# Low pieces of 23 operand blocks made beside attention and kept in DRAM, and the last product of attention's first pair in a bank of its own

## The chip, the cores and the metric

The kernel runs on one core of a Trainium2 chip. The metric is the device time of one execution in microseconds. The kernel before took 1278.0 us, the median of three runs (1276.09 to 1281.77).

## The reference

One decoder layer on a sequence of 1024 tokens with 1024 channels, all in float32. A single projection feeds two branches, the recurrence (Mamba-2) and forgetting attention; each branch goes through a 1024x1024 weight, the two are merged by gates, and the merged result goes through an output weight.

```python
h = _rmsnorm(x, pre_g)
proj = jnp.einsum('bld,de->ble', h, w_in)
z_ssm, xbc, dt_raw, q, k, v, f_raw, z_att, g_ssm, g_att = jnp.split(proj, _offsets(IN_SPLITS), axis=-1)
...
y_ssm = (yg.reshape(bsz, seqlen, SSM_D_INNER) * ssm_norm_g.astype(f32)).astype(x.dtype)
...
o = _forgetting_attention(heads(q), heads(k), heads(v), log_f)
o = o.transpose(0, 2, 1, 3).reshape(bsz, seqlen, ATT_D)
y_att = (o.astype(f32) * jax.nn.silu(z_att.astype(f32))).astype(x.dtype)
p_ssm = jnp.einsum('ble,ed->bld', y_ssm, w_branch_ssm)
p_att = jnp.einsum('ble,ed->bld', y_att, w_branch_att)
merged = jax.nn.sigmoid(g_ssm) * p_ssm + jax.nn.sigmoid(g_att) * p_att
out = jnp.einsum('bld,de->ble', merged, w_out)
return x + _rmsnorm(out, post_g)
```

## The kernel before

Every large matrix product is done by a seven-product scheme (Strassen and Winograd's). The activations, 1024 channels by 1024 tokens, are cut into four blocks of 512x512, b11, b12, b21 and b22, and from these come t1 = b12 - b11, t2 = b22 - t1, t3 = t2 - b11 and t4 = t2 - b21. Seven operands meet the weights: b11, b21, -b22, t1, -t2, t3, t4, held in SBUF as tiles x0 to x6 in this order. Each operand has four tiles of 128x512 (j = 0 to 3). TensorE multiplies in float32r, so each operand tile is split in two: a high piece (x3h, a rounded copy made by ScalarE) and a low piece (x3l, what the rounding lost, made by VectorE). One product is 4 x 3 = 12 matmuls of 128x512: high by high, high by low, low by high.

A `Pair` (L320) is two units of 128 output columns that share the seven products. Its steps have the numbers 1 to 7: step 1 uses b11 (x0), 2 b21 (x1), 6 -t2 (x4), 5 t1 (x3), 7 t3 (x5), 4 t4 (x6), 3 -b22 (x2). Steps 1, 6, 7 and 4 accumulate one after another into one PSUM bank, `self.b`; after 1, 6 and 7 ScalarE copies the bank to SBUF (`keep`, L399) before the next step may go on in it, because the sums in between are wanted too. `give` (L405) combines a bank with such a copy. `Stream` (L461) holds one list of steps for all 48 pairs: 36 of the input projection, then 4 of the recurrence's branch (weights `wbs`, operands `ops_s`), 4 of attention's branch (`wba`, `ops_a`) and 4 of the output weight (`ops_w`). A step is issued in two halves, and between halves the other work of the program is put: first the recurrence, then attention.

Attention (from L1322) runs 48 groups of 128-query blocks beside the stream: scores on TensorE (`s`), VectorE adds the forget gate and takes the row limit (`ex`, `nm`, L1505), ScalarE exponentiates (L1509), TensorE transposes (`pt`), ScalarE, for some tiles VectorE, copies that to SBUF (`p`, L1548 and L1546), TensorE multiplies by the values (`av`). Beside it, small steps called chores are taken from a line, one at each half.

`Operands.differences` (L197) is such a line of chores for `ops_s`: for each j it loads blocks of the recurrence's output, GpSimd subtracts (L211), and t1 to t4 are stored to DRAM on GpSimd's queue (L193). When a pair that uses other operands is next, `some` (L294) loads the new operands tile by tile (`fetch`, L257) into the low piece's place, and splits them (`split`, L265: ScalarE at L275 or L278, then VectorE at L276 or L279). For the output weight's operands t3, t4 and b22 the low pieces are already made early and kept in DRAM (`lows`): there `fetch` loads both pieces and `split` has only ScalarE's rounding in place (L269). Attention's own differences are made where its outputs appear (`outputs`, L1575). The last head pair's tiles are split straight from SBUF (`put`, L287).

`gp`, the pool of `small()` tiles (name `th`), has four buffers that go round among gates, loads and stores. The order on TensorE is that of the program; on the other engines a scheduler sets the order, except where `pin` keeps it.

## Time and profile before

| what | us |
|---|---|
| median of three runs | 1278.0 |
| the profiled execution | 1273.87 |
| its span | 1272.2 |
| TensorE busy | 1246.1 |
| VectorE busy | 1012.9 |
| ScalarE busy | 794.3 |
| GpSimd busy | 319.3 |

Attention lies between about 682 and 1122 us from the start of the span. The operands of the recurrence's branch are exchanged between about 918 and 977 us, those of attention's branch between about 1067 and 1130 us, those of the output weight between about 1170 and 1205 us. In a row of a view, `[0.69 <-ACT s L402]` means that the engine sat idle for 0.69 us before this instruction, until ScalarE's instruction at line 402 released it. PE is TensorE, PEld its weight loads, DVE VectorE, ACT ScalarE, POOL GpSimd, SP the engine that issues most loads. TensorE's matmuls overlap in the pipeline and their ends are modelled, so a product is best timed from start to start.

### The profile page before, as it was taken

How to read it: one execution, taken by the hardware profiler on the slowest of the kernel's cores; microseconds unless marked ns; L12 is line 12 of the kernel's file. 1: busy time of each engine (PE TensorE's matmuls, PEld its weight loads, DVE VectorE, ACT ScalarE, POOL GpSimd, SP SyncE). 2: the span in 40 equal slices, each digit the busy share in tenths (PEclk: the TensorE clock that was granted, in tenths of full speed). 3: DMA queues.
4: the chain of work that ended last, by engine and by line, in shares of the span. 5: the costliest groups of instructions: out<-in, count | busy, mean ns of one | idle time of the engine just before them, and what ended most of it. 6: DMA issues, size and time to landing. Idle time of an engine off the chain costs nothing.

```text
span 1272.2 us, 20822 instructions
## 1 busy us (share of the span) xinstructions
PE 1246.1 (98%) x6926; PEld 982.3 (77%) x6926; DVE 1012.9 (80%) x1994; ACT 794.3 (62%) x1737; POOL 319.3 (25%) x322
## 2 busy tenths in 40 slices
PE   5999999999999999999999999999999999999997
PEld 3678888888888888888887777777777777778886
DVE  7988886988888978997767676767789767886975
ACT  7745665556665765566555666666687666844753
POOL 4000440013400241115102124223112212356062
PEclk9999999999999999999999999999999999999999
DMA  8232452545436533744447576666687657766933
GB/s 300 69 120 76 146 162 88 191 152 182 138 101 215 175 127 117 219 146 140 142 149 252 162 228 212 217 214 218 232 286 263 224 184 249 249 221 199 364 110 105
DMA packets 152236, 233.56 MB, mean 184 GB/s; under 512 B 15201, under 2 KB 60737, under 8 KB 152129
## 3 DMA queue, kind: packets, MB, share of 16 engines
q1 hardware_dynamic: 136064, 196.08, 47.7%
q10 hardware_dynamic: 10560, 18.06, 3.8%
q0 software_dynamic: 5504, 18.09, 3.7%
q8 instruction: 54, 0.88, 0.3%
q14 instruction: 54, 0.43, 0.1%
HBM read 162.99 MB, written 72.34 MB: 185 GB/s over the span
## 4 chain that ended last, share of the span: by engine, by line
PE 86%; DMA 4%; DVE 4%; ACT 4%; issue 1%; SPq 0%; POOL 0%; DVEq 0%; ACTq 0%; POOLq 0%
PE pb L128 36%; PE pc L128 21%; PE pd L128 7%; PE av L128 5%; PE pt L131 5%; PE s L128 5%; PE yps L128 2%; PE st L128 1%; ACT ex L1509 1%; DMA xt<-in_x 1%; PE tr L131 1%; PE tr_v L131 1%; DMA v<-v_dram 1%; PE df L128 1%; DVE wop L350 1%
## 5 line engine op out<-in xcount | busy, mean ns | idle before, releaser
L350 DVE TENSOR_TENSOR wop<-sum,wop 128x512 fp32r<-128x512 f32 x180 | 140.2, 780 | 53.6 <-ACT wop L349 52.6
L349 ACT ACTIVATE wop<-sum 128x512 fp32r<-128x512 f32 x180 | 112.5, 626 | 109.0 <-DVE sum L355 52.4
L1509 ACT ACTIVATE ex<-ex,nm 128x512 f32<-128x512 f32 (+1 forms) x192 | 116.2, 606 | 71.9 <-DVE nm L1505 71.6
L402 ACT ACTIVATE s<-pb 128x512 f32<-128x512 f32 x144 | 85.3, 593 | 98.2 <-PE pb L128 96.2
L128 PE MATMUL pb<-x0h,wop 128*128 128x512 f32 x384 | 131.5, 399 | 0.0
L128 PE MATMUL pb<-x6h,wop 128*128 128x512 f32 x384 | 129.5, 395 | 1.3 <-ACT s L402 1.3
L128 PE MATMUL pb<-x5h,wop 128*128 128x512 f32 x384 | 130.1, 396 | 0.7 <-ACT s L402 0.7
L350 DVE TENSOR_TENSOR wop<-raw,wop 128x512 fp32r<-128x512 f32 x144 | 105.4, 733 | 31.8 <-ACT wop L349 31.5
L128 PE MATMUL pc<-x3h,wop 128*128 128x512 f32 x384 | 129.8, 396 | 0.5 <-DVE ot L419 0.4
L128 PE MATMUL pc<-x2h,wop 128*128 128x512 f32 x384 | 130.2, 397 | 0.0
L128 PE MATMUL pb<-x4h,wop 128*128 128x512 f32 x384 | 129.1, 395 | 0.0
L1505 DVE CUSTOM_DVE_ANT_0 ex<-s,fb 128x512 f32<-128x512 f32 (+1 forms) x192 | 96.8, 552 | 20.0 <-PE s L128 14.8
L349 ACT ACTIVATE wop<-raw 128x512 fp32r<-128x512 f32 x144 | 89.7, 623 | 14.7 <-PE pd L128 6.1
L128 PE MATMUL pd<-x1h,wop 128*128 128x512 f32 x288 | 96.3, 394 | 0.0
L128 PEld LDWEIGHTS pb<-x6h,wop 128*128 128x128 f32 x384 | 72.1, 188 | 18.6 <-issue 2.0
L128 PEld LDWEIGHTS pb<-x5h,wop 128*128 128x128 f32 x384 | 72.1, 188 | 18.4 <-issue 2.0
L128 PEld LDWEIGHTS pb<-x0h,wop 128*128 128x128 f32 x384 | 72.6, 189 | 17.6 <-issue 2.9
L128 PEld LDWEIGHTS pc<-x3h,wop 128*128 128x128 f32 x384 | 72.1, 188 | 17.7 <-issue 1.5
L128 PEld LDWEIGHTS pc<-x2h,wop 128*128 128x128 f32 x384 | 72.1, 188 | 17.4 <-issue 2.4
L128 PEld LDWEIGHTS pb<-x4h,wop 128*128 128x128 f32 x384 | 72.1, 188 | 16.7 <-issue 1.9
L211 POOL TENSOR_TENSOR wd<-wd 128x256 f32<-128x256 f32 x32 | 32.4, 1011 | 205.0 <-DMA wd<-in_wo 135.0
L131 PE MATMUL pt<-ident,ex 128*128 128x128 f32 x576 | 75.1, 273 | 2.0 <-ACT ex L1509 1.4
(318 smaller groups left out, 2993.6 us busy)
## 6 DMA issues: line engine op xcount, KB each, us to landing
raw<-in_wu SPq DMA_DIRECT2D x128, 256.0 KB
csb<-cs_dram SPq DMA_DIRECT2D x32, 256.0 KB
q<-q_dram SPq DMA_DIRECT2D x32, 256.0 KB
k<-k_dram SPq DMA_DIRECT2D x16, 512.0 KB
fb<-f_dram SPq DMA_DIRECT2D x16, 512.0 KB
rb<-st_dram SPq DMA_DIRECT2D x48, 128.0 KB
wd<-in_wo SPq DMA_DIRECT2D x40, 128.0 KB
xt<-in_x SPq DMA_DIRECT2D x8, 512.0 KB
```

Source lines behind the costliest of these rows:

```text
L128: return tc.keep_in_program_order(nc.tensor.matmul(*args, **kw))
L131: return tc.keep_in_program_order(nc.tensor.transpose(out_, in_, idn))
L211: pin(nc.gpsimd.tensor_tensor(t[out_], t[a_], t[b_], ALU.subtract))
L349: nc.scalar.activation(op[:, 0], src, AF.Copy)
L350: nc.vector.tensor_tensor(op[:, 1], src, op[:, 0], ALU.subtract)
L402: nc.scalar.activation(s, ps, AF.Copy)
L1505: nc.vector.tensor_tensor_reduce(o, s[e][:, 0:w], fb[hp, h][:, e, 0:w], 1.0, 3.0e38, ALU.add, ALU.min, nm)
L1509: pin(nc.scalar.activation(o, o, AF.Exp, scale=-1.0, bias=nm, accum_out=hd.at(hd.sm, i, h, e)))
```

## The change

Three edits. First, `ops_s` keeps low pieces of t1, t3, t4 and b22 (16 tiles), and `ops_a` those of t1 and t4 (seven tiles; the eighth, of the last head pair, is still split from SBUF). A new function `lower` makes them where the difference is at hand: ScalarE rounds into a `small()` tile, VectorE subtracts in place, GpSimd's queue stores it. A tile counts as ready once its low piece is stored. Second, `fetch` then loads two tiles for each of these, and `split` does ScalarE's rounding in place alone. Third, in attention's first pair step 7 gets a PSUM bank of its own: it doesn't wait for the copy of the sum of steps 1 and 6; VectorE adds that copy afterwards in `keep`, and step 4 goes on in the new bank and is combined in `give`.

The edit of `p.bank` for pairs behind that one has no effect: the banks of the last eight pairs are set anew behind attention, before these use them.

```diff
@@ class Operands
-            self.lows = {}
+            self.lows, self.late = {}, ()
         def ready(self, name, j):
-            if name in self.BLOCKS:
+            if name in self.BLOCKS and name not in self.late:
                 r, h = self.BLOCKS[name]
                 return self.there(KH * r + j, h)
             return (name, j) in self.made
         def store(self, name, j, t, cols=slice(0, HALF)):
             pin(self.queue.dma_start(self.dram[name][j][:, cols], t))
-            if cols.stop == HALF:
+            if cols.stop == HALF and name not in self.late:
                 self.made.add((name, j))
+        def lower(self, name, j, t):
+            s = small()
+            pin(nc.scalar.activation(s.bitcast(F32R), t, AF.Copy, scale=-1.0 if name == "b22" else 1.0))
+            if name == "b22":
+                pin(nc.vector.scalar_tensor_tensor(s.bitcast(F32R), t, -1.0, s, ALU.mult, ALU.subtract))
+            else:
+                pin(nc.vector.tensor_tensor(s.bitcast(F32R), t, s, ALU.subtract))
+            pin(self.queue.dma_start(self.lows[name][j], s))
+            self.made.add((name, j))
@@ differences
             wait = (None,) * room
+            if self.late:
+                part = lambda name, t: lambda: self.lower(name, j, state[t])
+                behind = lambda *fns: lambda: [fn() for fn in fns]
+                yield from (start, *wait, less("t1", "x", "x", "y"), keep("b22"), part("t1", "x"), None)
+                yield from (behind(part("b22", "y"), less("t2", "x", "y", "x")), keep("b11"), *wait)
+                yield from (less("t3", "y", "x", "y"), keep(), part("t3", "y"), lambda: fetch("b21"), *wait)
+                yield from (less("t4", "x", "x", "y"), keep(), part("t4", "x"))
+                return
@@ split
-            if name.strip("-") in self.lows:
+            if raw is None and name.strip("-") in self.lows:
@@ class Pair
+            self.apart = None
+        def another(self):
+            pool, tag = self.room
+            return pool.tile([P, HALF], F32, tag=tag, bufs=1, name="p" + tag)
-        def keep(self, ps):
+        def keep(self, ps, more=None):
             s = wp.tile([P, HALF], F32, tag="s", bufs=3, name="s")
             with tc.high_priority():
+                if more is not None:
+                    nc.vector.tensor_tensor(s, ps, more, ALU.add)
+                    return s
                 nc.scalar.activation(s, ps, AF.Copy)
@@ give
-                else:
+                elif how == "from":
                     nc.vector.tensor_tensor(d, s, ps, ALU.subtract)
+                else:
+                    nc.vector.scalar_tensor_tensor(d, ps, -1.0, s, ALU.mult, ALU.subtract)
@@ do
-                    yield from self.matmuls(self.b, 7, "t3", False)
-                    self.k7 = self.keep(self.b)
+                    if self.apart == 7:
+                        self.b = self.another()
+                    yield from self.matmuls(self.b, 7, "t3", self.apart == 7)
+                    self.k7 = self.keep(self.b, self.k2 if self.apart == 7 else None)
...
-                yield from self.matmuls(self.b, 4, "t4", False)
-                self.give(1, 0, self.b)
+                if self.apart == 4:
+                    self.b = self.another()
+                yield from self.matmuls(self.b, 4, "t4", self.apart == 4)
+                self.give(1, 0, self.b, {7: self.k2, 4: self.k7}.get(self.apart), "neither")
@@ class Stream
-                p.bank, p.other = (pj, "be"[n % 2]), (pjx, "d") if n < double else (pj, "c")
+                p.bank, p.other = (pj, "be"[(n + (n > last)) % 2]), (pjx, "d") if n < double else (pj, "c")
             a, b, c, d, e, f, g, h = pairs[last:]
+            a.apart, a.room = 7, (pj, "be"[(last + 1) % 2])
@@ the operands
+    ops_a.late = ("t1", "t4")
+    ops_a.lows = {n: tc.dram_tile([KH, P, HALF], F32, name=f"{n}_low_a") for n in ops_a.late}
+    ops_s.late = ("t1", "t3", "t4", "b22")
+    ops_s.lows = {n: tc.dram_tile([KH, P, HALF], F32, name=f"{n}_low_s") for n in ops_s.late}
@@ outputs
-                        stream.chores += [None, lambda: ops_a.store("t1", hp, y)]
+                        stream.chores += [None, lambda: ops_a.store("t1", hp, y), lambda: ops_a.lower("t1", hp, y)]
...
-                stream.chores += [None, lambda: ops_a.store("t4", j, x)]
+                stream.chores += [None, lambda: ops_a.store("t4", j, x), lambda: ops_a.lower("t4", j, x)]
```

The scheduled program changes from attention on; up to there every engine has the same instructions in the same order. Three places show how.

ScalarE, where the recurrence's operands are exchanged (x5 is t3 and x3 is t1 of `ops_s`; the line numbers of the changed kernel are higher). Before:

```order
L278 ACTIVATE x5h<-x5l 128x512 x2
L1509 ACTIVATE ex,sm<-ex,nm 128x512 x2
L1509 ACTIVATE ex,sm<-ex,nm 128x384
L413 ACTIVATE th<-pb 128x512
L349 ACTIVATE wop<-raw 128x512
L1509 ACTIVATE ex,sm<-ex,nm 128x384
L278 ACTIVATE x5h<-x5l 128x512 x2
L629 ACTIVATE th<-th 128x512
L278 ACTIVATE x3h<-x3l 128x512
L1431 ACTIVATE st<-pt 8x128
L1548 ACTIVATE p<-pt 128x2x128
L278 ACTIVATE x3h<-x3l 128x512
```

Now:

```order
L288 ACTIVATE x5h<-x5h 128x512 x2
L1547 ACTIVATE ex,sm<-ex,nm 128x512 x2
L1547 ACTIVATE ex,sm<-ex,nm 128x384 x2
L288 ACTIVATE x5h<-x5h 128x512 x2
L440 ACTIVATE th<-pb 128x512
L369 ACTIVATE wop<-raw 128x512
L1469 ACTIVATE st<-pt 8x128
L1586 ACTIVATE p<-pt 128x2x128
L1586 ACTIVATE p<-pt 128x512 x2
L663 ACTIVATE th<-th 128x512
L288 ACTIVATE x3h<-x3h 128x512 x2
```

The roundings are as many as before, but the second exponential of 384 columns no longer stands behind a gate's copy and a weight's rounding, and the copies `p` stand ahead of the roundings of x3.

ScalarE in attention's early part, where the first low piece is made (L200 is the rounding in `lower`). Before:

```order
L349 ACTIVATE wop<-sum 128x512
L1431 ACTIVATE st<-pt 8x128
L629 ACTIVATE th<-th 128x512
L1432 DMA st_dram<-st 8x128
L1548 ACTIVATE p<-pt 128x512
```

Now:

```order
L369 ACTIVATE wop<-sum 128x512
L663 ACTIVATE th<-th 128x512
L664 DMA gs_dram<-th 128x512
L200 ACTIVATE th<-x 128x512
L1469 ACTIVATE st<-pt 8x128
L1470 DMA st_dram<-st 8x128
L1586 ACTIVATE p<-pt 128x512
```

A rounding now stands ahead of a copy `p`. Of the 23 new roundings 12 stand ahead of a copy `p` with no exponential between.

TensorE at the end of attention, where step 6 (x4) of attention's first pair is followed by step 7 (x5). Before, the last row of step 6 and the first of step 7:

```order
L128 MATMUL pb<-x4h,wop 128x512
L128 MATMUL pb<-x5h,wop 128x512
L128 MATMUL pb<-x5l,wop 128x512
L128 MATMUL pb<-x5h,wop 128x512 x2
L128 MATMUL pb<-x5l,wop 128x512
```

Now:

```order
L128 MATMUL pb<-x4h,wop 128x512
L128 MATMUL pe<-x5h,wop 128x512
L128 MATMUL pe<-x5l,wop 128x512
L128 MATMUL pe<-x5h,wop 128x512 x2
L128 MATMUL pe<-x5l,wop 128x512
```

TensorE's order is the same; only the bank of steps 7 and 4 is another.

More of the change, by code (lines that the diff above doesn't have):

```diff
@@ L417, in give @@
                     nc.vector.tensor_tensor(d, ps, s, ALU.subtract)
+                elif how == "from":
+                    nc.vector.tensor_tensor(d, s, ps, ALU.subtract)
                 else:
-                    nc.vector.tensor_tensor(d, s, ps, ALU.subtract)
+                    nc.vector.scalar_tensor_tensor(d, ps, -1.0, s, ALU.mult, ALU.subtract)
             post(ch)
```

## The prediction

> **What bounds the kernel now.** I read the page first, busy time and the chain of work that ended last, then the busy time by stretch, then the waits of TensorE, and last the timeline where TensorE stood still.
>
> ```profile
> PE 1246.1 (98%) x6926; PEld 982.3 (77%) x6926; DVE 1012.9 (80%) x1994; ACT 794.3 (62%) x1737; POOL 319.3 (25%) x322
> PE 86%; DMA 4%; DVE 4%; ACT 4%; issue 1%; SPq 0%; POOL 0%; DVEq 0%; ACTq 0%; POOLq 0%
> 1142.50 8.16 PE pb L128 x36
> ```
>
> TensorE is busy for 98% of the span and holds 86% of the chain. The third row, from the chain in order of time, gives its pace: 36 matmuls in 8.16 us, 2.72 us a product. The change leaves the number and the order of matmuls alone, so it can win only where TensorE waits, and lose only by new waits of TensorE. The busy time by stretch shows where it waits (columns: PE, PEld, DVE, ACT, POOL busy, granted clock, DMA share, GB/s):
>
> ```profile
> 683.00:945.00 262.00, 261.24 (x1768) 198.39 (x1764) 188.22 (x505) 175.47 (x445) 68.55 (x86) 1.00 0.64 213
> 945.00:960.00 15.00, 13.73 (x85) 9.05 (x85) 14.73 (x34) 11.71 (x28) 2.15 (x4) 1.00 0.98 352
> 960.00:980.00 20.00, 19.62 (x128) 14.61 (x125) 18.25 (x46) 15.88 (x40) 4.68 (x6) 1.00 0.69 228
> 1105.00:1125.00 20.00, 18.72 (x103) 13.69 (x104) 18.66 (x38) 15.54 (x36) 6.98 (x6) 1.00 0.72 231
> 1125.00:1150.00 25.00, 25.00 (x112) 20.72 (x111) 20.25 (x23) 8.78 (x16) 18.28 (x13) 1.00 0.57 178
> ```
>
> In the 262 us of attention ahead of the exchange of operands TensorE stands for 0.76 us. It stands for 1.27 and 0.38 us at the exchange to the recurrence's branch, where VectorE is busy 98% and 91% of the time, and for 1.28 us at attention's end. Behind that it doesn't stand at all. The reader is to see that both places are where VectorE is full, and that the prize is small: 2.93 us of visible idle time.
>
> A busy TensorE can hide a little more. The timeline, with TensorE and its weight loads, shows it:
>
> ```profile
> 951.29 0.14 PEld L131 LDWEIGHTS pt<-ident,ex 128*128 128x128 f32 x1 [0.39 <-DVE nm L1505]
> 953.69 0.53 PEld L131 LDWEIGHTS pt<-ident,ex 128*128 128x128 f32 x5 [1.17 <-ACT ex L1509]
> 955.76 2.87 PE L128 MATMUL s<-k,q 64*128 64x512 f32 x12
> 977.26 0.30 PEld L128 LDWEIGHTS s<-k,q 64*128 64x128 f32 x4 [0.82 <-DVE p L1546]
> 1095.46 1.50 PE L128 MATMUL s<-k,q 64*128 64x512 f32 x12
> 1112.96 0.19 PEld L128 LDWEIGHTS pc<-x3l,wop 128*128 128x128 f32 x1 [0.66 <-DVE x3l L279]
> 1113.90 0.19 PEld L128 LDWEIGHTS pc<-x3l,wop 128*128 128x128 f32 x1 [0.41 <-DVE x3l L279]
> 1120.45 0.19 PEld L128 LDWEIGHTS pb<-x5h,wop 128*128 128x128 f32 x1 [1.11 <-ACT s L402]
> ```
>
> The twelve score matmuls take 2.87 us at 955.76 and 1.50 us at 1095.46, so 1.37 us of the first are a wait. With the idle time of the weight loads the exchange costs 0.39 + 1.17 + 1.37 + 0.82 = 3.75 us, and attention's end 0.66 + 0.41 + 1.11 = 2.18 us. Together 5.9 us are the most that the change can win.
>
> **The change part by part.** First, the splits that go from the exchange. These are VectorE's, and what stands about them:
>
> ```profile
> L279 DVE TENSOR_TENSOR x3l<-x3l,x3h 128x512 fp32r<-128x512 f32 x8 | 5.3, 684 | 1.2 <-ACT x3h L278 1.2
> 951.63 0.68 DVE L279 TENSOR_TENSOR x5l<-x5l,x5h 128x512 fp32r<-128x512 f32 x1
> 952.42 0.62 ACT L349 ACTIVATE wop<-raw 128x512 fp32r<-128x512 f32 x1
> 975.58 1.28 DVE L276 SCALAR_TENSOR_TENSOR x2l<-x2l,x2h 128x512 fp32r<-128x512 f32 x2
> 976.78 0.42 DVE L1546 COPY p<-pt 128x256 f32<-128x256 f32 x1
> ```
>
> Sixteen of 0.684 us leave VectorE between 950 and 977, 10.9 us, and seven leave attention's end, 4.8 us. ScalarE's roundings stay, as many as before. I go through the four waits. The one at 951.29 is for a row limit behind a split of x5: it goes (0.4). The one at 953.69 is for an exponential that stood behind a gate's copy and the rounding of a weight; in the new order it stands ahead of both, and I count 0.9 of 1.17. The one at 955.76 is for copies `p` that stood behind roundings of x3 and now stand ahead; 1.0 of 1.37. At 977.26 TensorE waits for VectorE's copy at 976.78, which came behind two splits of x2 that go: 0.7 of 0.82. Sum 3.0 us, from 0 (ScalarE alone still holds them) to 3.75.
>
> At attention's end the waits at 1112.96 and 1113.90 are for low pieces of x3 that VectorE made just then; they now come from DRAM, and the last high piece was rounded ahead of the product's second half:
>
> ```profile
> 1111.26 0.62 ACT L278 ACTIVATE x3h<-x3l 128x512 fp32r<-128x512 f32 x1
> ```
>
> Both waits go, 1.0 us.
>
> Second, the bank. Step 7 (x5) stood 1.11 us for the copy of the bank that step 6 had just left. In a bank of its own it needs only its operands. Its last low piece must be there for the product's eleventh matmul, 10 x 8.16 / 36 = 2.27 us into it:
>
> ```profile
> 1118.68 0.68 DVE L279 TENSOR_TENSOR x5l<-y,x5h 128x512 fp32r<-128x512 f32 x1
> 1119.80 0.60 ACT L402 ACTIVATE s<-pb 128x512 f32<-128x512 f32 x1 [1.32 <-PE pb L128]
> 1121.09 0.68 DVE L1463 TENSOR_TENSOR zr<-o,rb 128x512 f32<-128x512 f32 x1
> 1124.10 0.68 DVE L279 TENSOR_TENSOR x1l<-zr,x1h 128x512 fp32r<-128x512 f32 x1
> 1126.02 0.39 PE L128 MATMUL pd<-x1h,wop 128*128 128x512 f32 x1
> ```
>
> The piece was done at 1119.36 and comes earlier with four splits fewer ahead of it. So 1.0 us of 1.11 is won. Next late would be x1's last piece: done at 1124.78, needed 2.27 us into the product of x1, which began at 1126.02, so at 1128.3. If all is 2 us earlier on TensorE it is needed at 1126.3, 1.5 us behind the old time of the piece; the store of the last head's scales now stands behind two roundings on ScalarE (some 1.2 us later), and the added sum of step 7 stands ahead of the piece on VectorE (0.68), against the splits that went. I call this even, with up to 1 us to lose. The sum moved from ScalarE to VectorE costs about 0.7 us there twice, beside a TensorE that never stands behind 1125. End: 2.0 us won, from 1.0 to 2.18.
>
> Third, what is added in attention: 23 roundings on ScalarE (0.62 each), the same 23 subtractions on VectorE (0.684), 23 stores of 256 KB on GpSimd and 23 loads more on SP. VectorE sits idle 262 - 188 = 74 us of the first stretch above and ScalarE 87 us; 20 of the tiles put 13.7 and 12.4 us there. That fits on average. What decides is where a rounding stands. TensorE's scores wait for ScalarE's copies `p`, whose banks they take:
>
> ```profile
> PEld s L128 <- ACT p L1548: 4.9, 14, 0.4
> ACT p L1548 <- PE pt L131: 8.9, 11, 1.3
> ACT ex L1509 <- DVE nm L1505: 38.3, 35, 3.0
> L278 ACT ACTIVATE x3h<-x3l 128x512 fp32r<-128x512 f32 x8 | 4.6, 616 | 0.0
> ```
>
> These are waits of the same 262 us, some 29 groups of attention (48 groups in 440 us are about 9 us each). In 14 of 29 the scores wait for a copy; in 11 ScalarE itself was idle ahead of a copy, and takes a rounding for nothing. Twelve of the 23 roundings stand ahead of a copy with no exponential between; the others stand ahead of exponentials, which wait for VectorE anyway (35 times, 1.1 us each), and I count them as hidden. So 12 x 14/29 x 18/29 x 0.616 = 2.2 us lost. From below the bound is nothing; from above every one of the 20 in that stretch holds TensorE for its length, 12.3 us. I take 2.2, since even the short waits of today are 0.35 us each.
>
> On GpSimd a store waits for the subtraction, and behind it stand the differences and the masks of the forget gates (L1373), for which VectorE waited 1.4 us ahead of its widest shape in the whole run (first row below). I count nothing, up to 2 us. The loads:
>
> ```profile
> L1505 DVE CUSTOM_DVE_ANT_0 ex<-s,fb 128x512 f32<-128x512 f32 x96 | 61.8, 685 | 10.1 <-PE s L128 8.6 <-POOL fb L1373 1.4
> ...
> t_s<-x POOLq DMA_DIRECT2D x12, 256.0 KB, 3.0
> t_a<-y POOLq DMA_DIRECT2D x4, 256.0 KB, 6.2
> 972.75 0.40 PE L128 MATMUL pb<-x5h,wop 128*128 128x512 f32 x1
> 1200.00:1205.00 5.00, 5.00 (x23) 3.88 (x22) 3.36 (x7) 5.00 (x12) 1.07 (x1) 1.00 1.05 405
> ```
>
> Sixteen loads more are 4.2 MB into a stretch where the DMA share is 0.98 at 352 GB/s; at the 405 GB/s of the last row they take 10.4 us. That row is the same edit at work for the output weight, twelve tiles in two pieces with the queues full, and TensorE ran at 5.00 of 5.00. Operands are split well ahead of their product (x5l at 951.63 above, its product at about 972, 20 us later), so I count nothing here, up to 2 us for the loads of the scales `rb` behind them. [...]
>
> The sum: 3.0 + 2.0 - 2.2 = 2.8, so about 3 us won. The profiled execution took 1273.87 us, its span 1272.2 and 1.67 around it; it would be 1271. The median of the runs shown is 4.1 us above that execution, so the time I predict is 1278.0 - 3 = **1275 us**.
>
> **The rivals.**
>
> *ScalarE's roundings land on TensorE.* In attention each rounding pushes a copy `p` or an exponential, and TensorE waits for its whole length. For it: 12 of the new ones stand straight ahead of copies, and the waits above show these are on the edge. Against: 87 us of idle ScalarE. It decides from the point where more than 8 of 20 land in full (8 x 0.616 = 5). All 20: 1278 + 12.3 - 5.0 = 1285 us, slower.
>
> *The exchange doesn't profit.* ScalarE keeps its 16 roundings and the loads double, so the waits between 950 and 977 stay under other names; attention's end wins 2.0, attention loses 2.2: 1278 us. For it: three of the four waits involve ScalarE. Against: the new order of ScalarE.
>
> *The stores hold the tiles.* `small` has four buffers, and one store keeps its buffer until it lands, 3.0 to 6.2 us behind the issue above. A gate's VectorE instruction waits for a buffer once today:
>
> ```profile
> DVE th L419 <- DMA gs_dram<-th: 1.7, 1, 1.7
> ```
>
> With 23 users more it could be five times, 8.5 us with all behind it on VectorE: 1278 + 8.5 - 2.8 = 1284 us. [...]
>
> *All of it is won and nothing lost:* 1278 - 5.9 = 1272 us. For it: the idle shares. Against: the twelve places.
>
> That the splits don't leave the exchange is excluded by the new order; that the bank edit changes nothing is not, if step 7 then waits for x5's last piece, and is in the range.
>
> **How the numbers follow.** My forecast has 0.50, the exchange without profit 0.20, all won 0.14, ScalarE's roundings 0.11, the held tiles 0.05. What a measurement of this kernel can tell from no change is about 0.5%, 6.4 us. Faster by more needs more than the 5.9 us that I see, so only some hidden wait or noise gives it: 0.10, most of it from "all won". Slower by more, over 1284.4, is a good half of the two slow cases and what noise adds from the others: 0.13. Within: 0.77. The range takes the all-won case with 3 us for the runs' own spread (1276.09 to 1281.77) and reaches up to the two slow cases: 1269 to 1284. The forecast's own range is 1272 to 1277.
>
> **What would show it.** VectorE's splits of x2, x3, x5 and x6 between 950 and 977 gone, and TensorE idle there under 0.6 us instead of 1.65; no wait of x5's first matmul for ScalarE's copy; 23 roundings of `th` in attention, and TensorE's waits for `p` in the first stretch grown from 4.9 to about 7 us. I'm wrong if those waits grow by over 8 us, if VectorE waits for buffers `th` many times, or if the idle time at the exchange stays.

## The result, and the profile after

| | us | ratio to before, 95% interval |
|---|---|---|
| before, median of 6 | 1277.7 (1276.09 to 1281.77) | |
| the change, median of 6 | 1300.76 (1296.53 to 1302.7) | 1.0172 (1.0152 to 1.0193) |
| its profiled execution, and span | 1300.57, 1298.9 | |

The change is 22 us slower (19 to 25, the interval times 1277). 1275 was predicted, with a range from 1269 to 1284. The page of the change, busy time and the shares of the chain of work that ended last:

```profile
PE 1259.8 (97%) x6926; PEld 989.0 (76%) x6926; DVE 1015.8 (78%) x1996; ACT 805.1 (62%) x1758; POOL 326.0 (25%) x345
...
PE 66%; DVE 11%; DMA 10%; ACT 6%; issue 5%; POOL 1%; SPq 1%; ACTq 0%; DVEq 0%; POOLq 0%
```

The span grew by 26.7 us, from 1272.2; the profiled execution of before lay 3.8 us under its median, so the 22 us of the medians are the better size. TensorE is busy 13.7 us longer with the same 6926 matmuls, and stands 13.0 us longer. In the chain it fell from 86% to 66%, and VectorE, transfers and ScalarE took its place: TensorE now waits for them. The first stretch of attention, and three pairs of short stretches inside and behind it (columns: PE, PEld, DVE, ACT, POOL busy, granted clock, DMA share, GB/s):

```profile
683.00:945.00 262.00, 251.39 (x1641) 187.83 (x1641) 185.20 (x485) 172.28 (x429) 75.07 (x100) 0.98 0.65 218
878.30:881.71 3.41, 1.32 (x9) 0.96 (x9) 3.34 (x11) 2.48 (x7) 2.43 (x3) 1.00 0.56 195
881.71:888.54 6.83, 5.69 (x22) 4.10 (x22) 3.09 (x11) 3.24 (x8) 1.24 (x3) 0.50 0.47 153
939.74:943.15 3.41, 0.78 (x4) 0.41 (x5) 3.41 (x11) 3.04 (x8) 0.58 (x2) 1.00 0.91 266
943.15:946.56 3.41, 3.41 (x15) 3.29 (x16) 3.38 (x7) 3.41 (x10) 1.71 (x2) 0.50 0.73 272
1127.48:1130.89 3.41, 1.60 (x9) 0.78 (x7) 0.83 (x2) 1.89 (x6) 2.92 (x3) 1.00 0.90 314
1130.89:1137.72 6.83, 6.68 (x31) 4.53 (x32) 3.55 (x14) 4.56 (x14) 0.56 (x1) 0.50 0.32 104
```

Before, TensorE was busy 261.24 of the first 262 us and did 1768 matmuls there. Now it is busy 251.39 and does 1641. The other rows show that the loss is not spread evenly: TensorE stands for half to three quarters of 3.41 us, and the next 3.41 or 6.83 us run at half the clock. Before, the granted clock was 1.00 in every stretch that the prediction shows. The three slow pieces are 17.1 us; TensorE is busy for 15.8 of them. From 885.20, in the first piece, matmuls of 128x512 start 0.42 us apart, and from 947.13, behind the second, 0.23 us. So the three cost at most about half of the 15.8, 7.9 us, which is an estimate from these figures.

Who is waited for in the same 262 us (waits: us in total, times, longest), first before, then the change:

```profile
PEld pt L131 <- ACT ex L1509: 1.7, 4, 0.5
...
ACT th L644 <- DMA za_dram<-th: 1.0, 1, 1.0
...
DVE th L419 <- DMA st_dram<-st: 0.8, 1, 0.8
```

```profile
PEld pt L131 <- ACT ex L1547: 11.8, 12, 3.4
...
DVE th L204 <- ACT th L200: 10.3, 10, 2.2
...
PEld s L128 <- ACT p L1586: 5.3, 13, 1.1
...
ACT th L200 <- DMA gs_dram<-th: 2.2, 1, 2.2
...
DVE th L446 <- DMA ga_dram<-th: 2.1, 1, 2.1
DVE th L444 <- DMA st_dram<-st: 2.0, 1, 2.0
...
ACT th L200 <- DMA t_low_s<-th: 1.5, 1, 1.5
...
DVE th L446 <- DMA gs_dram<-th: 1.3, 1, 1.3
```

In the change L200 is `lower`'s rounding, L204 its subtraction, L205 its store. TensorE's waits for ScalarE's copies `p`, on which the prediction laid the loss, went from 4.9 to 5.3 us. The waits that grew are others. TensorE's transposes wait for the exponentials: 1.7 us became 11.8 at the weight loads (0.5 became 8.1 at the matmuls, largely in the same gaps). Ahead of that stand two kinds of waits. VectorE's subtraction stands ten times for ScalarE's rounding (10.3 us), which is new. And five waits of more than a microsecond are for a tile `th` that a store still holds (9.1 us), where before had three such waits of 1.7, 1.0 and 0.8 us (a tile of the scales, `st`, comes from the same four). One place shows both, in order of time:

```profile
875.47 0.69 DVE L444 TENSOR_TENSOR th<-pc,s 128x512 f32<-128x512 f32 x1 [2.00 <-DMA st_dram<-st]
876.20 0.63 ACT L663 ACTIVATE th<-th 128x512 f32<-128x512 f32 x1 [2.66 <-DVE th L444]
...
877.23 0.63 ACT L200 ACTIVATE th<-y 128x512 fp32r<-128x512 f32 x1 [0.40 <-ACT th L663]
877.90 0.69 DVE L204 TENSOR_TENSOR th<-y,th 128x512 fp32r<-128x512 f32 x1 [0.41 <-ACT th L200]
...
879.23 0.72 ACT L1547 ACTIVATE ex<-ex,nm 128x512 f32<-128x512 f32 x1 [1.37 <-DVE nm L1543]
...
880.10 0.20 PEld L131 LDWEIGHTS pt<-ident,ex 128*128 128x128 f32 x2 [2.32 <-ACT ex L1547]
```

VectorE's combination of a product (L444) finds no free tile and stands 2.00 us for the store of a head's scales. The gate on ScalarE comes late by it, the rounding stands behind the gate, the subtraction behind the rounding, and the row limits of the next scores stand on VectorE behind the subtraction. The exponentials come late, TensorE waits 2.32 us and, at 883.22, another 1.49, and between the two the clock falls to half. The second pair of stretches begins alike:

```profile
937.46 0.69 DVE L446 TENSOR_TENSOR th<-s,pc 128x512 f32<-128x512 f32 x1 [2.06 <-DMA ga_dram<-th]
...
942.09 0.20 PEld L131 LDWEIGHTS pt<-ident,ex 128*128 128x128 f32 x2 [3.39 <-ACT ex L1547]
```

Between these rows stand a gate, a rounding (939.22), its subtraction (939.88) and the row limits (940.50), as above. Ahead of the third pair ScalarE's copy of the scales stood 1.52 us for a tile (1129.03). So a wait for a tile stands ahead of each of the three falls of the clock, and in two of them the added work stands in line behind it. The third is only in part the tile's: TensorE's matmuls stood 1.72 us there, and 1.03 us at the same place in the run with the loads only, further down, where that copy stood for no tile.

### The profile page after: what moved, and what is told of

It is laid out like the page before. It is cut to its first block, busy times and chain, and to the rows that moved or that the text cites. A ratio compares the mean times of both kernels' runs of the same rounds, so it can differ in the third digit from the quotient of the medians.

```text
span 1298.9 us, 20951 instructions
## 1 busy us (share of the span) xinstructions
PE 1259.8 (97%) x6926; PEld 989.0 (76%) x6926; DVE 1015.8 (78%) x1996; ACT 805.1 (62%) x1758; POOL 326.0 (25%) x345
## 4 chain that ended last, share of the span: by engine, by line
PE 66%; DVE 11%; DMA 10%; ACT 6%; issue 5%; POOL 1%; SPq 1%; ACTq 0%; DVEq 0%; POOLq 0%
PE pb L128 28%; PE pc L128 16%; PE pd L128 5%; PE av L128 4%; PE pt L131 4%; PE s L128 3%; DVE wop L370 2%; PE yps L128 2%; ACT ex L1547 2%; DMA xt<-in_x 1%; DVE sum L375 1%; ACT wop L369 1%; DMA gs_dram<-th 1%; DMA raw<-in_wu 1%; DMA th<-ga_dram 1%
## 5 line engine op out<-in xcount | busy, mean ns | idle before, releaser
L128 PE MATMUL pb<-x5h,wop 128*128 128x512 f32 x376 | 127.3, 396 | 0.0
L131 PE MATMUL pt<-ident,ex 128*128 128x128 f32 x576 | 80.0, 280 | 9.6 <-ACT ex L1547 8.4
L128 PEld LDWEIGHTS pc<-x3h,wop 128*128 128x128 f32 x384 | 72.1, 188 | 18.3 <-issue 1.5
L131 PEld LDWEIGHTS pt<-ident,ex 128*128 128x128 f32 x576 | 67.9, 143 | 22.3 <-ACT ex L1547 13.0
L128 PEld LDWEIGHTS pb<-x5h,wop 128*128 128x128 f32 x376 | 70.6, 188 | 17.1 <-issue 2.0
```

Of the source, the lines that this page charges most:

```text
L128: return tc.keep_in_program_order(nc.tensor.matmul(*args, **kw))
L131: return tc.keep_in_program_order(nc.tensor.transpose(out_, in_, idn))
```

## The experiments

Times are medians. The third column of the table below is the ratio to the runs of the kernel before on the same chip, and the fourth that ratio's distance from 1 times 1277. "Late" are the 23 tiles whose low piece the change takes from DRAM.

| run | us | ratio, 95% interval | us against before |
|---|---|---|---|
| the bank alone | 1277.29 | 1.0008 (0.9994 to 1.0021) | +1.0 |
| late, no second load, no making | 1275.54 | 0.9981 (0.9968 to 0.9995) | -2.4 |
| the same, old bank | 1274.23 | 0.9978 (0.9967 to 0.9988) | -2.8 |
| late, second loads, no making | 1279.38 | 1.0013 (0.9996 to 1.0029) | +1.7 |
| and stores from a constant | 1279.76 | 1.0015 (1.0003 to 1.0028) | +1.9 |
| or the roundings alone | 1283.43 | 1.0052 (1.0028 to 1.0077) | +6.6 |
| or tiles that GpSimd fills and stores | 1285.65 | 1.0074 (1.0049 to 1.0100) | +9.4 |
| or the subtractions alone | 1287.57 | 1.0080 (1.0068 to 1.0092) | +10.2 |
| or both, with a step between them | 1288.51 | 1.0092 (1.0069 to 1.0116) | +11.7 |
| or both on VectorE | 1288.32 | 1.0100 (1.0074 to 1.0125) | +12.8 |
| or both as in the change, no stores | 1295.70 | 1.0143 (1.0117 to 1.0170) | +18.3 |
| the change | 1300.76 | 1.0172 (1.0152 to 1.0193) | +22.0 |
| the change, with a step between | 1300.76 | 1.0182 (1.0167 to 1.0196) | +23.2 |
| before, a fifth tile | 1279.65 | 1.0028 (1.0013 to 1.0043) | +3.6 |
| the change, a fifth tile | 1304.25 | 1.0206 (1.0183 to 1.0230) | +26.3 |
| the change, both | 1302.32 | 1.0200 (1.0180 to 1.0221) | +25.5 |

### The parts one by one

**The bank alone.** `late` and the calls of `lower` are taken out.

```diff
-    ops_a.late = ("t1", "t4")
...
-    ops_s.late = ("t1", "t3", "t4", "b22")
```

> Only the other bank for step 7 with its sums; no low pieces are made or loaded. Three theories for the 23 us that the change lost. A, held tiles: each low piece takes one of the four tiles th until its store has landed, and the gates, the scales and the loads that need such a tile wait in their queues. B, work in the chain: ScalarE's rounding and VectorE's subtraction stand ahead of the exponentials and the copies p. C, transfers: the doubled loads and the 23 stores fill the DMA engines. All three say that this part alone loses nothing: 1275 to 1278 us. Over 1285 us the bank is the cause and all three fall.

It took 1277.29 us: nothing won and nothing lost that can be told from noise. The timeline at attention's end shows why; step 7's wait of 1.11 us is gone, and this stands instead:

```profile
1128.05 1.62 POOL L375 TENSOR_TENSOR sum<-sum,raw 128x512 f32<-128x512 f32 x1 [1.28 <-issue]
...
1128.44 1.78 DVE L370 TENSOR_TENSOR wop<-raw,wop 128x512 fp32r<-128x512 f32 x1
...
1131.94 0.68 DVE L298 TENSOR_TENSOR x6l<-x6l,x6h 128x512 fp32r<-128x512 f32 x1
...
1132.67 0.19 PEld L128 LDWEIGHTS pe<-x6l,wop 128*128 128x128 f32 x1 [2.14 <-DVE x6l L298]
```

TensorE now waits 2.14 us for the last low piece of x6, three products on. That piece comes when VectorE comes to it; VectorE is full there (busy for all of the 8 us from 1125 to 1133), and a weight's split ahead of it took 1.78 us beside GpSimd's sum, where the one at 1121.32, with GpSimd idle, took 0.68. Here all of x6 is still split by VectorE, so the run prices the bank without the late operands, not beside them.

**The loads alone.** The pieces are not made; where one would be loaded, the raw block is loaded a second time.

```diff
+            again = self.copy(KH * r + j, c) if block in self.BLOCKS else self.dram[block][j]
...
             if block in self.lows:
-                nc.sync.dma_start(self.tiles[name][1][:, j, :].bitcast(F32), self.lows[block][j])
+                low = again if self.late else self.lows[block][j]
+                nc.sync.dma_start(self.tiles[name][1][:, j, :].bitcast(F32), low)
...
@@ lower
-            s = small()
...
-            pin(self.queue.dma_start(self.lows[name][j], s))
             self.made.add((name, j))
```

> The change without the making of the low pieces: no rounding, no subtraction, no tile, no store; where a low piece would be loaded the raw block is loaded a second time, so the loads are the change's and the splits leave the exchange (the output lacks the low pieces). A (held tiles) and B (work in the chain): the exchange and the bank are won and nothing is lost, 1272 to 1276 us. C (transfers): most of the loss stays, over 1288 us.

**Made, but not stored**, and **held, but not made**. Both start from the run above. The first puts the rounding and the subtraction back, without the store; in the second GpSimd fills a tile and stores it:

```diff
+            s = small()
+            pin(nc.gpsimd.memset(s, 0.0))
+            pin(self.queue.dma_start(self.lows[name][j], s))
```

> As the run with the loads only, but the low pieces are made: 23 roundings and 23 subtractions into a tile th, which is not stored, so a tile is free again about 2 us after it is taken (the raw block is loaded a second time in place of the low piece). B (work in the chain): 1293 to 1301 us, as the change. A (held tiles): 1275 to 1281 us. C: as the run with the loads only.

> As the run with the loads only, but each piece takes a tile th that GpSimd fills with zeros and stores, so the tile is held until its store lands, and ScalarE and VectorE have no work for it (the raw block is loaded a second time in place of the low piece). A (held tiles): 1288 to 1300 us. B (work in the chain): 1272 to 1279 us. C: the run with the loads only and up to 6 us for the stores.

1279.38, 1295.70 and 1285.65 us. Transfers are not the cause of the large loss, though they ate what the late splits should win. The making without stores loses 16.6 us over the loads alone (18.3 - 1.7), so the work decides more than the hold by a store; but a tile that only GpSimd touches loses 7.7 us as well. Neither theory came out alone. That last run's waits in the same 262 us:

```profile
PEld pt L131 <- ACT ex L1545: 5.2, 7, 1.6
...
DVE th L444 <- DMA gs_dram<-th: 2.3, 1, 2.3
```

With no work added to ScalarE or VectorE, the exponentials come late all the same (5.2 us, before 1.7): a combination stands 2.3 us for a tile.

**The exchange without second loads.** As the loads alone, with one load, and the low piece filled with zeros by GpSimd at the split; then the same with the old bank.

```diff
-                nc.sync.dma_start(self.tiles[name][1][:, j, :].bitcast(F32), low)
+                if not self.late:
+                    nc.sync.dma_start(self.tiles[name][1][:, j, :].bitcast(F32), low)
@@ split
+                if self.late:
+                    pin(nc.gpsimd.memset(l.bitcast(F32), 0.0))
```

```diff
-            a.apart, a.room = 7, (pj, "be"[(last + 1) % 2])
```

> As the run with the loads only (1279.4 us), but without the second loads of the late operands: at the split GpSimd fills the low piece with zeros, so ScalarE's roundings stay, VectorE's splits are gone and the traffic is that of before (the output lacks the low pieces). If the doubled loads, which fill the DMA engines between 945 and 980 us and hold up the loads queued behind them on SP, ate the exchange's gain: 1271 to 1275 us, and TensorE's wait for the copies p at about 977 us is gone. If ScalarE's roundings alone hold the exchange: 1277 to 1280 us, as with the loads.

> As the run without second loads (1275.5 us), with the old bank for step 7. If the bank wins its 1.0 us as predicted: 1276 to 1278 us. If step 7's wait only covered the last head's outputs, which come when they come: no change, 1273 to 1276 us. The late splits' gain at the exchange, 3.0 us as predicted, and 1.0 at attention's end, would make 1273 to 1274 us against 1277.2.

1275.54 and 1274.23 us. Both have a flaw at attention's end, where GpSimd's fill comes late. With the new bank:

```profile
1129.91 0.19 PEld L128 LDWEIGHTS pe<-x6l,wop 128*128 128x128 f32 x1 [2.85 <-POOL x6l L284]
```

TensorE stands 2.85 us here and 1.42 us once more for this stand-in, and 0.96 us in the run with the old bank. So the two times tell the least that the late splits can win, and their difference doesn't price the bank. The busy time by stretch, of the run with one load and of that with two:

```profile
945.00:960.00 15.00, 15.00 (x97) 10.70 (x97) 13.94 (x32) 13.43 (x32) 4.57 (x10) 1.00 0.97 329
960.00:980.00 20.00, 20.00 (x131) 15.26 (x128) 13.30 (x40) 17.21 (x44) 9.62 (x18) 1.00 0.91 302
```

```profile
945.00:960.00 15.00, 15.00 (x94) 10.81 (x94) 10.80 (x23) 13.27 (x30) 2.00 (x4) 1.00 1.01 356
960.00:980.00 20.00, 17.98 (x115) 13.27 (x111) 13.07 (x38) 14.08 (x35) 3.29 (x7) 1.00 1.01 362
```

With one load TensorE stands at neither place (before, it stood 1.27 and 0.38 us). With two, the DMA share is 1.01 for 35 us, and a new gap of 2.02 us stands in the second stretch. Its timeline:

```profile
978.85 0.69 DVE L1103 SCALAR_TENSOR_TENSOR th<-th 128x512 f32<-128x512 f32 x1 [1.18 <-DMA th<-gs_dram]
...
979.92 0.42 DVE L1579 COPY p<-pt 128x256 f32<-128x256 f32 x1 [0.38 <-ACT st L1464]
...
980.40 0.18 PEld L128 LDWEIGHTS s<-k,q 64*128 64x128 f32 x1 [2.44 <-DVE p L1579]
```

A gate's load, issued at 975.71, comes late behind the pairs of loads of x2 on SP's queue; VectorE stands 1.18 us for it, ScalarE's copy of the scales stands behind VectorE, the copies `p` behind that, and the scores wait 2.44 us. The change has the same gap at 998.86 us, of 2.46 us. The run has a second place, at attention's end:

```profile
1132.15 0.69 DVE L1496 TENSOR_TENSOR zr<-o,rb 128x512 f32<-128x512 f32 x1 [4.20 <-DMA rb<-st_dram]
...
1135.29 0.19 PEld L128 LDWEIGHTS pd<-x1l,wop 128*128 128x128 f32 x1 [1.55 <-DVE x1l L293]
```

VectorE stands 4.20 us for the last head's scales, and x1's pieces are late by it: SP stood 5.9 us until the store of these scales had landed (3.3 us before, 4.8 us with one load, so the second loads are not shown to be the whole cause). The granted clock is 0.91 from 980 to 1000 us and 0.83 from 1130 to 1140. This profiled execution took 1283.74 us, the longest of its ten, so its gaps are at the large end. By the medians the second loads cost about 4 us (+1.7 against -2.4, the difference known to some 3 us), and with them the exchange wins nothing.

**The stores without a tile.** As the loads alone, with the 23 stores at the change's places, but from a constant.

```diff
+            s = ident.unsqueeze(1).to_broadcast([P, 4, P])
+            pin(self.queue.dma_start(self.lows[name][j].rearrange("p (a b) -> p a b", a=4), s))
```

> As the run with the loads only (1279.4 us), with 23 stores of 256 KB on GpSimd's queue at the places of the change's, but from a constant, so that no tile th is taken and no engine works for them (the output lacks the low pieces). The run with tiles that GpSimd filled and stored took 1285.7 us. If that price is the held tile: 1279 to 1282 us here. If it is the stores' traffic and their places on GpSimd's queue: 1284 to 1287 us.

1279.76 us, as the loads alone (1279.38). Stores and their places on GpSimd's queue cost nothing that can be seen; the exponentials are on time, and a tile is waited for twice, 1.4 us together (with the loads only twice, 1.2 us; waits in the same 262 us):

```profile
PEld pt L131 <- ACT ex L1544: 1.8, 4, 0.6
...
ACT th L675 <- DMA za_dram<-th: 1.2, 1, 1.2
...
DVE th L443 <- DMA st_dram<-st: 0.2, 1, 0.2
```

The 7.7 us of the filled tiles are therefore the tile's, or GpSimd's filling's, which itself stood for tiles. VectorE took as long beside the filling as with the loads only (the row limits 552 ns on average in both, the weights' splits `wop<-sum,wop` 770 and 767 ns), so the tile is the likelier; no run has the one without the other.

### The work taken apart

All four start from the run that made the pieces without storing them. The first leaves out the subtraction. The second leaves out the rounding, the third puts a copy on VectorE in its place:

```diff
-            pin(nc.scalar.activation(s.bitcast(F32R), t, AF.Copy, scale=-1.0 if name == "b22" else 1.0))
...
+            pin(nc.vector.tensor_tensor(s.bitcast(F32R), t, t, ALU.subtract))
```

```diff
-            pin(nc.scalar.activation(s.bitcast(F32R), t, AF.Copy, scale=-1.0 if name == "b22" else 1.0))
+            pin(nc.vector.tensor_copy(s.bitcast(F32R), t))
```

In the fourth the rounding stays, and the subtraction is called one chore later:

```diff
+            def rest():
+                pin(nc.vector.tensor_tensor(s.bitcast(F32R), t, s, ALU.subtract))
...
+            self.rest = rest
@@ differences, and alike for the others
-                yield from (start, *wait, less("t1", "x", "x", "y"), keep("b22"), part("t1", "x"), None)
+                yield from (start, *wait, less("t1", "x", "x", "y"), keep("b22"), part("t1", "x"), lambda: self.rest())
```

> As the run that made the pieces without storing them (1295.7 us; the run with the loads only took 1279.4), but with ScalarE's 23 roundings alone: VectorE's subtractions are left out. B1, the rounding itself stands ahead of the exponentials and the copies on ScalarE: 1290 to 1296 us. B2, VectorE stands in its order for ScalarE's rounding and makes the row limits late: 1279 to 1284 us. B3, ScalarE waits for a free tile th ahead of the rounding: 1290 to 1296 us, with waits of the roundings for stores in the trace.

> As the run with the loads only (1279.4 us), with 23 instructions of VectorE of the subtraction's size into a tile th that isn't stored, and no rounding on ScalarE (the output lacks the low pieces). The rounding alone added 4 us, both with a step between them 9, both back to back 16. If work and hand-off add up: 1282 to 1286 us, and about 7 us are the hand-off's own. If VectorE's work alone is the price of both: 1292 us or more.

> As the run that made the pieces without storing them (1295.7 us), but VectorE makes the rounding too, with a copy ahead of its subtraction, so that neither engine waits for the other; ScalarE has nothing added. B1 (ScalarE's rounding): 1279 to 1285 us. B2 (VectorE waits for ScalarE): 1280 to 1286 us, since two VectorE instructions take about what the wait and one took. If VectorE's work itself is the price: 1292 to 1300 us. B3 (waiting for a tile): 1290 to 1296 us, now with VectorE's waits.

> As the run that made the pieces without storing them (1295.7 us), with the same work, but the subtraction stands one step of the work around behind its rounding, so that ScalarE has finished when VectorE comes to it. B2 (VectorE waits for ScalarE): 1280 to 1287 us. B1 (ScalarE's rounding) and B3 (waiting for a tile): no change, 1292 to 1299 us.

1283.43, 1287.57, 1288.32 and 1288.51 us. Over the loads alone that is 4.9 for the roundings, 8.5 for the subtractions, 10 for both with a step between, 11 for both on VectorE, and 16.6 back to back. Only the roundings' time lies in a range that was expected for one cause (B2); the other three lie between the ranges. The order in which the two stand is worth some 6 us without stores (16.6 against 10, each known to about 3 us), and hardly by way of the tiles: the engines stood 6.2 us for tiles in the 262 us of the run back to back, and 6.1 us in the run with a step between. The waits of the run with a step between, same 262 us, show it:

```profile
PE s L128 <- DVE p L1589: 5.1, 3, 4.0
...
ACT st L1474 <- DMA ga_dram<-th: 2.3, 1, 2.3
...
PEld pt L131 <- ACT ex L1552: 1.6, 3, 0.7
```

TensorE's waits for exponentials are back at 1.6 us. What is left is one wait of 4.0 us for a copy `p` behind the copy of the scales, which stood 2.3 us for a tile; the granted clock of this profiled execution was 0.994, against 0.999 before. In the run with the subtractions alone VectorE stood 2.3 us for a tile too, at 870 us, ahead of the exponentials. Each stand-in took a tile `th`, so these prices hold some of the tile's.

### Ways to mend the whole change

**A step between, in the whole change** (with the store behind the subtraction).

> The whole change, with each subtraction (and its store) one step of the work around behind its rounding, so that VectorE doesn't stand in its order for ScalarE. If that wait is the largest part of the loss, as the runs without stores say (1295.7 us with it, 1288.5 without): some 7 us less than the change, 1292 to 1296 us, and TensorE's waits of pt for ex fall from 21 us to under 8 us between 690 and 1150. If the stores and held tiles decide whatever the order: 1298 to 1303 us.

1300.76 us, as the change: what the step wins without stores is lost with them. The waits in the same 262 us:

```profile
DVE th L448 <- DMA t_low_s<-th: 3.6, 1, 3.6
...
ACT st L1473 <- DMA ga_dram<-th: 2.3, 1, 2.3
DVE th L206 <- ACT th L200: 2.3, 2, 1.9
```

VectorE's waits for roundings fell from 10.3 to 2.3 us and TensorE's for exponentials only from 11.8 to 8.7 us. A combination now stands 3.6 us for a tile that a low piece's own store holds, and the scales 2.3 us, and the granted clock of the profiled execution was 0.991, against 0.992 in the change. A step more between rounding and store is a step more in which the tile is held.

**Tiles of their own**, with the memory of a fourth weight buffer.

```diff
-            op = wp.tile([P, 2, KH, P], F32R, tag="wop", bufs=4, name="wop")
+            op = wp.tile([P, 2, KH, P], F32R, tag="wop", bufs=3, name="wop")
...
-            s = small()
+            s = gp.tile([P, HALF], F32, tag="lo", bufs=2, name="lo")
```

> The kernel before with three instead of four buffers for the split weights, which frees 4 KB a partition for the next two runs. It is their control: the products' weights are made one step less ahead. 1277 to 1290 us; what it adds is taken off the next two.

> The whole change with three weight buffers, and two tiles of their own for the low pieces, so that they never take one of the four tiles th. A (held tiles; the pieces and the work that was put in place of them all took such a tile): at least 14 of the change's 23 us gone, 1279 to 1287 us plus what the control adds over 1277. B (the added work and VectorE's wait for ScalarE): 1293 to 1298 us plus what the control adds; only the stores' hold, 5 us, goes.

> As the run with own tiles, with each subtraction one step behind its rounding. With tiles of their own a longer hold costs nothing. If VectorE's wait for ScalarE has a price apart from the tiles: 4 to 8 us less than the run with own tiles. If the tiles were all: the same within 2 us.

1386.44 for the control, then 1389.57 and 1394.89 us (1.085, 1.087 and 1.0917 of before). The weight buffer is worth 108 us by itself (0.085 x 1277). The two others lie 3 and 8 us above it, but a kernel that waits for weights all along hides other waits, so this told nothing of the tiles.

**A fifth tile.** q goes from two buffers to one, each of its loads moves to the last place ahead of its use, and the scales `rb` get the 2 KB.

```diff
-            t = ap.tile([P, 2, 256], F32R, tag="q", bufs=2, name="q")
+            t = ap.tile([P, 2, 256], F32R, tag="q", bufs=1, name="q")
...
-                rb = self.rb[n] = small("rb")
+                rb = self.rb[n] = ap.tile([P, HALF], F32, tag="rb", bufs=1, name="rb")
@@ loads
             if g == 1:
-                load_q(hp, (3, 2))
+                load_q(hp, (5, 4))
...
```

> The kernel before with one buffer for q instead of two, each load moved to the last place ahead of its use, and the 2 KB so won given to the scales rb, which held one of the four tiles th before. It is the control for the next two runs: before hardly waits for tiles (1.7 us once), so a fifth tile wins at most 1 to 2 us, and late q can lose some: 1275 to 1283 us.

> The whole change with that fifth tile. A (held tiles): most of the waits for tiles go, and the loss over the control falls from 23 us to 10 or less: 1283 to 1291 us with a control of 1278. B (the added work in the order of ScalarE and VectorE): the loss over the control stays at 18 to 24 us, 1296 to 1302 us.

> The whole change with the fifth tile and each subtraction one step behind its rounding, which without the tile took 1300.8 us, as the change. If the step's gain (7 us in the runs without stores) was given back by the longer hold of the tiles: 5 to 8 us less than the change with the fifth tile. A alone: as the change with the fifth tile. B alone, with the order the largest part: 1291 to 1295 us.

1279.65, 1304.25 and 1302.32 us. Over its control the change loses 22.7 us (26.3 - 3.6), as without the tile; with the step between 21.9. But this tile has a price that its control hardly pays: TensorE stands for q, which now has one buffer. First all of attention, then the 262 us:

```profile
PE s L128 <- DMA q<-q_dram: 8.0, 5, 2.2
```

```profile
DVE th L446 <- DMA ga_dram<-th: 2.0, 1, 2.0
DVE th L446 <- DMA t_a<-y: 2.0, 1, 2.0
```

The waits for q are 8.0 us (6.6 with the step between), in the control 1.3. So what the tile may have won was paid for with late q, and the 22.7 us don't refute the held tiles. Nor was one tile enough to take the waits for tiles away: four of 7.2 us together are left, against 9.1. The run shows that this fifth tile doesn't mend the change, not what the tiles cost.

**What stays open:** the shares of the two. That the order of the work costs something where no piece is stored is shown (16.6 against 10 us), that a tile held by a store costs something, with GpSimd's filling of it, is shown (7.7 against 0 us for the same stores from a constant), and that neither mend, nor both together, brings the whole change back. A run with no wait for tiles at all was not had: each tile more was bought with another buffer, and late weights or late q may hide what it won. No version beats both kernels: the only two runs below before, by under 3 us, leave the low pieces out.

## Why the prediction was wrong

**What bounds the kernel: right.** TensorE's waits alone decided. That at most 5.9 us could be won held too: with all costs left out, 2.4 to 2.8 us were won, in runs that still stood up to 4.3 us for a stand-in.

**The exchange, 3.0 us won: right in mechanism, given back by the loads.** With one load TensorE is busy 35.00 of 35 us there, and the whole run gains 2.8 us (1.5 to 4.2) with the old bank. But "I count nothing here, up to 2 us" for the doubled loads was mis-sized: about 4 us. The row that I leaned on, twelve tiles in two pieces at 405 GB/s with TensorE at 5.00 of 5.00, lay where no attention ran beside it. I asked whether operands come in time for their products, and they do; late was a gate's load queued behind them, with the scales and the copies `p` behind that. The scales `rb`, for which I allowed up to 2 us, were late too, at attention's end, where VectorE stood 4.20 us for them. The 405 GB/s was not held over the exchange: the 35 us with the queues full show 356 and 362 GB/s at a share of 1.01.

**Attention's end, 2.0 us won: half of it wrong.** The two waits for x3 are gone wherever operands are late. The bank alone gave nothing. I looked for what is late next and named x1's last piece and VectorE's 0.68 us, and called it even. In the run with the bank alone it is x6's, one product later, by 2.14 us, on a VectorE that is full and that took 1.78 us for a weight's split beside GpSimd's sum. With late operands it is x1's, as named, by 1.55 us with the loads only and by 0.70 us in the change. What the bank is worth beside late operands stays open.

**The added work, 2.2 us lost: the step that failed.** "[T]he others stand ahead of exponentials, which wait for VectorE anyway [...] and I count them as hidden." The exponentials wait for VectorE, and VectorE now waits for ScalarE's rounding: what I took for cover is the path. I priced ScalarE's 12 roundings ahead of copies `p`, where the waits grew by 0.4 us, and gave VectorE's 23 subtractions room on average (74 us idle). Here the subtractions took up more than their own 0.69 us each: ten of those in the first stretch brought their operand's wait, 10.3 us, to all that stood behind them. Measured: 16.6 us over the loads alone, some 6 of them by the order of the two, and my bound from above, 12.3, was too low too, since it counted ScalarE's time alone.

**The held tiles: named, priced at 8.5 us, and given 0.05.** "[W]aits for a buffer once today" was one row of three: before already stood 3.5 us for tiles in the first stretch. Five such waits there, 9.1 us, are what that rival said ("it could be five times, 8.5 us"). The chance was too small: 23 more users of four tiles, each held until its store has landed, should have been the first thing to count. The change's transfers (`--dma`) show most of their stores, with the median from issue to landing last:

```profile
t_low_s<-th POOLq DMA_DIRECT2D x12, 256.0 KB, 3.6
...
t_low_a<-th POOLq DMA_DIRECT2D x7, 256.0 KB, 5.4
```

Of the stores that before has too, the same median went from 3.0 to 4.0 us for t_s<-x and from 5.9 to 5.6 for t_a<-y, while VectorE's busy share in attention fell from 75% (682 to 1122 us) to 72% (682 to 1148).

**GpSimd's queue and its stores, nothing: right as far as tested.** 1279.76 against 1279.38 us. But those stores wait for nothing, and the change's wait for a subtraction. VectorE's waits for GpSimd's masks in attention grew from 5.0 us (longest 2.4) to 9.0 us (longest 3.6); behind the longest TensorE stood under half a microsecond.

**ScalarE's roundings in full: near in size, off in kind.** 1285 us for it; the roundings alone took 1283.43. The two rivals on the slow side, added, would have said 1294 us (1278 + 12.3 + 8.5 - 5.0), still 7 short. I treated them as cases apart, though they meet on the same engines: a late tile makes a late gate, that a late rounding, that a late limit.

**What I did not see at all:** the three pieces at half clock, behind stretches in which TensorE stood up to 1.9, 3.0 and 1.7 us at a time; by the estimate above they hold up to 7.9 us of the 26.7.

## What to carry to other kernels

Work that is put into an engine's order costs what it waits for as well as what it takes (here 10.3 us of waits for roundings in 262 us): ask, for every added instruction, which engine makes its operand and what stands right behind it. Idle time on average (74 us of VectorE's here) is no cover where a chain of four engines turns over every nine us. Count the users of a shared ring of tiles by the time that each holds one, the landing of its store included (3.6 and 5.4 us here), before giving it 23 more.

## What the runs showed of the hardware

**Half the clock behind three short gaps.** In the profile of the change TensorE was busy for 1.32, 0.78 and 1.60 us of 3.41, and the granted clock was 0.50 for the next 6.83, 3.41 and 6.83 us. TensorE's longest single waits there were 1.9, 3.0 and 1.7 us. Between 683 and 1148 us of this profile, laid out in stretches of 3.41 us from where the pieces begin, TensorE was busy for 2.31 us or more in every other stretch at full clock, and the clock was 1.00 in the stretch behind each of them. In the profile of before, in stretches with the same bounds, the least was 2.48 us, and the clock was 1.00 in all.

**VectorE's subtractions beside GpSimd.** In the run with the bank alone a subtraction of two 128x512 tiles took 0.68 us (1131.94), and one that makes a weight's low piece took 1.78 us (1128.44) when GpSimd's sum of 1.62 us had started 0.39 us ahead of it; the next one for a weight took 1.77 us (1132.54) beside a GpSimd instruction of 1.66 us. Not all are long there: another one for a weight took 0.68 us (1123.73) beside a GpSimd sum that stands in the profile from 1123.05 for 3.72 us.
